# Rearranging keys and queries over the partitions: six and three copies, partly in place, instead of eight and four into new tiles

## The chip, the cores and the metric

The kernel runs on one core of a Trainium2 chip. The metric is the device time of one execution in microseconds (us). TensorE is called PE here, its weight loads PEld, VectorE DVE, ScalarE ACT, GpSimd POOL and SyncE SP. SP computes nothing: it issues DMA transfers from one queue, in order, and where one of them has to wait for a semaphore, SP waits with it.

## The reference

Two layers over 256 latent and 256 context tokens, width 1024. A layer is a half-step feed-forward block, a mix of three branches (neighbourhood attention, Fourier mixing, windowed grouped-query attention with sinks), and another half-step block. The part that the change touches is the two attentions:

```python
s_loc = jnp.einsum('brcqhd,brcwkhd->bhrcqwk', qg, kb).astype(jnp.float32) * scale + bias[None]
s_ctx = jnp.einsum('brcqhd,blhd->bhrcql', qg, kc).astype(jnp.float32) * scale
p = jax.nn.softmax(jnp.concatenate([s_loc, s_ctx], axis=-1), axis=-1)
...
w = window_gqa_attention(apply_rope(heads(wq, WA_HEADS), cos, sin), apply_rope(heads(wk, WA_KV_HEADS), cos, sin), ...)
```

There are eight heads of 64 channels in either attention, eight key heads in the first and two in the second. In the second layer only the latent tokens have queries.

## The kernel before

Everything is float32, but PE multiplies a rounded form of it. So each operand is split in two parts, `hi` (the rounded value) and `lo` (the rest), and a product is made of several matmuls: `mm3` (lines 293 to 295) does three for a projection, a score does two (lines 712 and 713).

Weights come as 424 blocks of 128x1024. For each, SP loads a `raw` tile (line 57, 512 KB), ACT makes `wh` (line 66), DVE or, inside attention, POOL makes `wl` (line 79). Five `raw` tiles are in rotation.

A projection of keys or queries gives a PSUM tile with two heads: the channels of one head in partitions 0 to 63 (called x in the code), those of the other in 64 to 127 (y). ACT writes its `hi` (line 876, or 896 behind the rotary embedding), DVE its `lo` (878 or 898). A score matmul contracts over 128 partitions, and the kernel fills them with both parts of one head: for queries a tile with `hi` above `lo`, for keys one tile with `hi` in both halves and one with `lo` in both halves. The first matmul of a score (712) multiplies the query tile by the `hi` keys, the second (713) by the `lo` keys. `stack` makes these tiles with DMA copies of 64 partitions from SBUF to SBUF (line 871): four for a pair of queries, eight for a pair of keys. Per layer there are five pairs of keys (four `nk`, one `wk`) and eight of queries (four `nq`, four `wq`).

Tiles of the tag `act` (activations, probabilities, `hi` and `lo` parts, stacked tiles, and temporaries named `tmp`) share 60 buffers. A new tile takes a buffer that an older one has left, and its first writer waits for the last reader of the old one.

The order of all instructions is written out by the program itself: `attention` walks through blocks of four scores, and between two steps `fill` puts in projection work according to a table of due times, and `pieces` runs the stages of the evacuations. The rotary embedding (`rope`) of `wk` and `wq` issues four small copies on SP (line 890), then three operations on POOL (893), then ACT (896), DVE (898) and `stack`. Loads of weights (57), of attention masks (697) and the copies all stand in SP's one queue in program order.

Of the kernel before, what the change touches and what calls it, by code (L numbers as in the profile page):

```python
# [7 lines left out]
F32 = mybir.dt.float32  # L8
# [255 lines left out]
class Emit:  # L264
# [568 lines left out]
    def mix(self, l, norm, nxt):  # L833
        nc, W = self.nc, self.W
        ctxq = l < DEPTH - 1
        n = NT if ctxq else NLAT
# [3 lines left out]
        u = norm.all()  # L840
# [4 lines left out]
        res, pending, later, items, spare, clock = {}, [], [], [], [], [0]  # L845
# [11 lines left out]
        def stack(name, hi, lo, n):  # L857


            a, b = self.act(), self.act()  # L860
            x, y = slice(0, 64), slice(64, 128)
            if "q" in name[0]:
                moves = (a, x, hi, x), (a, y, lo, x), (b, x, lo, y), (b, y, hi, y)
                res[name] = a, b
            else:
                c, d = self.act(), self.act()
                moves = ((a, x, hi, x), (a, y, hi, x), (b, x, hi, y), (b, y, hi, y),
                         (c, x, lo, x), (c, y, lo, x), (d, x, lo, y), (d, y, lo, y))
                res[name] = a, b, c, d
            for t, i, s, j in moves:  # L870
                nc.sync.dma_start(out=t[i, :n].bitcast(F32), in_=s[j, :n].bitcast(F32))

        def plain(scale):
            def evac(name, ps, n):
                hi, lo = self.act(), self.act()
                nc.scalar.activation(out=hi[:, :n], in_=ps[:, :n], func=AF.Copy, scale=scale)
                yield
                nc.vector.scalar_tensor_tensor(out=lo[:, :n], in0=ps[:, :n], scalar=scale,
                                               in1=hi[:, :n].bitcast(F32), op0=ALU.mult, op1=ALU.subtract)
                stack(name, hi, lo, n)  # L880
            return evac

        def rope(scale):
            def evac(name, ps, n):

                t, r = self.tmp()[:, :n], self.tmp()[:, :NLAT]
                nc.scalar.activation(out=t, in_=ps[:, :n], func=AF.Copy)
                for b in range(4):
                    o = 32 * (b ^ 1)
                    nc.sync.dma_start(out=r[32 * b:32 * b + 32], in_=t[o:o + 32, :NLAT])  # L890
                yield 2
                for x, y, z, op in ((t, t, self.cos, ALU.mult), (r, r, self.sin, ALU.mult), (t, t, r, ALU.add)):
                    nc.gpsimd.tensor_tensor(out=x[:, :NLAT], in0=y[:, :NLAT], in1=z, op=op)
                yield 1
                hi, lo = self.act(), self.act()
                nc.scalar.activation(out=hi[:, :n], in_=t, func=AF.Copy, scale=scale)
                yield 1
                nc.vector.scalar_tensor_tensor(out=lo[:, :n], in0=t, scalar=scale, in1=hi[:, :n].bitcast(F32),
                                               op0=ALU.mult, op1=ALU.subtract)
                stack(name, hi, lo, n)  # L900
            return evac
# [310 lines left out]
```

## Time and profile before

| | us |
|---|---|
| median of 3 runs | 2097.94 |
| lowest and highest | 2097.83, 2099.03 |
| the profiled execution | 2094.62 |
| its span | 2092.8 |
| PE busy in it | 2046.4 (98%) |
| DVE, ACT, POOL busy | 1269.2, 837.7, 370.0 |

The profiled execution is one execution of the program with the hardware profiler on; its span runs from its first to its last instruction, and all positions in this text are us from the start of that span. Layer 0 does its attention from about 485 to 650, layer 1 from about 1661 to 1775.

### The profile page before, as it was taken

To read this page: it belongs to the slowest core of one execution; us is meant where nothing else is said; L and a number is where in the kernel's file an instruction comes from. 1 tells how busy PE (TensorE), PEld (TensorE's weight loads), DVE (VectorE), ACT (ScalarE), POOL (GpSimd) and SP (SyncE) were. 2 spreads that over 40 slices of the span, in tenths; PEclk is the share of its full clock that TensorE was granted. 3 is DMA by queue.
4 is the path that set the end of the run, shared out by engine and by line. 5 is a ranking of instruction groups with operands and counts; after the bars stand their busy time and mean duration, and the time that the engine had idled before them with its cause. 6 is when DMAs were issued, how large, how long until landed. Compare 5 with 4: busy or idle time off the path is not lost.

```text
span 2092.8 us, 29113 instructions
## 1 busy us (share of the span) xinstructions
PE 2046.4 (98%) x11193; PEld 1764.3 (84%) x11193; DVE 1269.2 (61%) x2035; ACT 837.7 (40%) x1362; POOL 370.0 (18%) x373
## 2 busy tenths in 40 slices
PE   7999999999999999999999999999999999999998
PEld 3788888878887888988888898888888888999998
DVE  6777776565676335677777566533336558566554
ACT  4422222345787223442222243222224558645443
POOL 5200000402452111300000120000012157330002
PEclk8999999999999999999999999999999999999999
DMA  7456557445522333466666655633334474565553
GB/s 279 147 191 200 188 196 225 118 141 151 134 81 78 92 101 91 141 191 193 197 191 192 212 145 197 201 92 101 101 118 142 131 194 112 164 182 160 189 180 106
DMA packets 103011, 326.65 MB, mean 156 GB/s; under 512 B 13396, under 2 KB 18516, under 8 KB 102872
## 3 DMA queue, kind: packets, MB, share of 16 engines
q1 hardware_dynamic: 102872, 324.79, 50.0%
q8 instruction: 88, 1.44, 0.3%
q14 instruction: 51, 0.42, 0.1%
HBM read 305.60 MB, written 1.05 MB: 147 GB/s over the span
## 4 chain that ended last, share of the span: by engine, by line
PE 89%; DVE 5%; ACT 2%; DMA 1%; issue 1%; SPq 1%; POOL 1%; DVEq 0%; POOLq 0%; ACTq 0%
PE ps L294 27%; PE ps L295 27%; PE ps L293 27%; DVE dump L315 2%; PE ps L764 1%; PE ps L746 1%; PE ps L589 1%; PE ps L588 1%; PE ps L587 1%; DVE wl L79 1%; ACT wh L66 1%; PE ps L712 1%; PE ps L713 1%; ACT tmp L770 0%; DVE act L218 0%
## 5 line engine op out<-in xcount | busy, mean ns | idle before, releaser
L294 PE MATMUL ps<-act,wh 128*128 128x512 f32 (+1 forms) x3227 | 1121.6, 348 | 8.0 <-DVE act L233 7.3
L293 PE MATMUL ps<-act,wh 128*128 128x512 f32 (+1 forms) x3227 | 1122.6, 348 | 2.1 <-ACT act L212 1.1
L295 PE MATMUL ps<-act,wl 128*128 128x512 f32 (+1 forms) x3227 | 1120.5, 347 | 1.8 <-DVE wl L79 1.8
L294 PEld LDWEIGHTS ps<-act,wh 128*128 128x128 f32 x3227 | 613.7, 190 | 84.6 <-DVE act L233 8.8
L295 PEld LDWEIGHTS ps<-act,wl 128*128 128x128 f32 x3227 | 613.6, 190 | 77.5 <-DVE wl L79 2.6
L293 PEld LDWEIGHTS ps<-act,wh 128*128 128x128 f32 x3227 | 613.8, 190 | 77.0 <-ACT act L212 1.3
L66 ACT ACTIVATE wh<-raw 128x1024 fp32r<-128x1024 f32 x424 | 436.5, 1050 | 318.7 <-PE ps L294 283.3
L79 DVE TENSOR_TENSOR wl<-raw,wh 128x1024 fp32r<-128x1024 f32 x379 | 473.4, 1262 | 102.5 <-ACT wh L66 102.4
L315 DVE CUSTOM_DVE_ANT_0 dump<-ada,silu_row 128x1024 bf16<-128x1024 f32 x224 | 273.5, 1221 | 11.4 <-DMA ada<-in_w_ada 9.1
L302 ACT ACTIVATE act<-tmp 128x512 fp32r<-128x512 f32 (+1 forms) x122 | 66.8, 566 | 430.7 <-DVE tmp L517 412.5
L455 POOL TENSOR_TENSOR tmp<-h 128x512 f32<-128x512 f32 (+1 forms) x7 | 11.4, 1634 | 1121.3 <-DVE h L472 793.8
L472 DVE SCALAR_TENSOR_TENSOR h<-ps,mod,h 128x256 f32<-128x256 f32 x136 | 61.8, 481 | 200.0 <-PE ps L295 200.0
L517 DVE TENSOR_TENSOR tmp<-tmp,ps 128x512 f32<-128x512 f32 (+1 forms) x88 | 54.6, 620 | 206.3 <-PE ps L295 201.5
L79 POOL TENSOR_TENSOR wl<-raw,wh 128x256 fp32r<-128x256 f32 x180 | 142.5, 822 | 200.7 <-ACT wh L66 184.8
L303 DVE TENSOR_TENSOR act<-tmp,act 128x512 fp32r<-128x512 f32 (+1 forms) x122 | 74.3, 626 | 60.5 <-ACT act L302 60.5
L516 ACT ACTIVATE tmp<-ps 128x512 f32<-128x512 f32 (+1 forms) x88 | 47.8, 543 | 121.0 <-PE ps L295 120.3
L461 POOL TENSOR_TENSOR tmp<-h 128x256 f32<-128x256 f32 (+1 forms) x44 | 64.3, 1462 | 107.4 <-DVE h L472 103.0
L753 DVE TENSOR_TENSOR act<-ps,act 128x512 fp32r<-128x512 f32 x80 | 55.0, 687 | 33.8 <-ACT act L748 29.0
L724 ACT ACTIVATE tmp<-tmp,sm 128x512 f32<-128x512 f32 (+1 forms) x96 | 62.1, 647 | 31.5 <-DVE sm L722 30.0
L764 PE MATMUL ps<-act 128*128 128x256 f32 x320 | 61.6, 308 | 11.0 <-DVE act L753 9.4
L748 ACT ACTIVATE act<-ps 128x512 fp32r<-128x512 f32 x80 | 47.5, 594 | 45.9 <-PE ps L746 45.4
L1057 ACT ACTIVATE tmp<-ps 128x512 f32<-128x512 f32 (+1 forms) x30 | 15.4, 512 | 121.6 <-PE ps L295 121.6
(110 smaller groups left out, 1317.8 us busy)
## 6 DMA issues: line engine op xcount, KB each, us to landing
raw<-in_ws SPq DMA_DIRECT2D x424, 512.0 KB, 4.1
ada<-in_w_ada SPq DMA_DIRECT2D x128, 512.0 KB, 3.7
act<-act SPq DMA_DIRECT2D x112, 128.0 KB, 2.4
tmp<-in_w_ada_sc SPq DMA_DIRECT2D x16, 256.0 KB, 5.4
tmp<-in_w_ada SPq DMA_DIRECT2D x16, 256.0 KB, 6.0
masks<-in_na_bias SPq DMA_DIRECT2D x8, 512.0 KB, 5.0
h<-in_h SPq DMA_DIRECT2D x8, 256.0 KB, 5.3
act<-act SPq DMA_DIRECT2D x32, 64.0 KB, 4.2
```

The costliest lines, as they stand in the source:

```text
L66: self.nc.scalar.activation(out=wh, in_=self.raw[i], func=AF.Copy)
L79: self.lo_engine.tensor_tensor(out=wl[:, s], in0=raw[:, s], in1=self.hi[i][:, s].bitcast(F32), op=ALU.subtract)
L293: mm(ps, lhsT=w[0], rhs=x[0], start=start, stop=False)
L294: mm(ps, lhsT=w[0], rhs=x[1], start=False, stop=False)
L295: mm(ps, lhsT=w[1], rhs=x[0], start=False, stop=stop)
L302: nc.scalar.activation(out=hi, in_=src, func=AF.Copy)
L303: nc.vector.tensor_tensor(out=lo, in0=src, in1=hi.bitcast(F32), op=ALU.subtract)
L315: self.nc.vector.tensor_tensor_reduce(out=self.dump[:, ks], in0=w, in1=self.silu_row[:, v, ks], scale=1.0, scalar=m if half else 0.0, op0= ...
L461: nc.gpsimd.tensor_tensor(out=sq, in0=h, in1=h, op=ALU.mult)
L472: self.nc.vector.scalar_tensor_tensor(out=h, in0=ps, scalar=self.mod[l, g][:, v, j:j + 1], in1=h, op0=ALU.mult, op1=ALU.add)
L724: nc.scalar.activation(out=e[:, :nk], in_=e[:, :nk], func=AF.Exp, scale=-1.0, bias=nm, accum_out=b["sum"][:, i:i + 1])
L764: nc.tensor.matmul(b["ps"][hp][:, :256], lhsT=v, rhs=t[j][:, cs], start=c == 0 and j == 0, stop=c == n - 1 and j == 1)
```

## The change

`stack` keeps the two tiles that ACT and DVE wrote and uses them as half of its results. For a pair of queries it takes one new tile `b`, copies `hi`'s and `lo`'s lower half (y) into it, and then writes `lo`'s upper half over `hi`'s lower half; that third copy overwrites what the first one reads. For a pair of keys it takes two new tiles and does, once for `hi` and once for `lo`: lower half to the new tile's upper half, lower half to the new tile's lower half, then the old tile's upper half over its own lower half. Nothing else is changed.

```diff
-            a, b = self.act(), self.act()
             x, y = slice(0, 64), slice(64, 128)
+
+            def move(t, i, u, j):
+                nc.sync.dma_start(out=t[i, :n].bitcast(F32), in_=u[j, :n].bitcast(F32))
+
+            b = self.act()
             if "q" in name[0]:
-                moves = (a, x, hi, x), (a, y, lo, x), (b, x, lo, y), (b, y, hi, y)
-                res[name] = a, b
+                move(b, x, hi, y)
+                move(b, y, lo, y)
+                move(hi, y, lo, x)
+                res[name] = hi, b
             else:
-                c, d = self.act(), self.act()
-                moves = ((a, x, hi, x), (a, y, hi, x), (b, x, hi, y), (b, y, hi, y),
-                         (c, x, lo, x), (c, y, lo, x), (d, x, lo, y), (d, y, lo, y))
-                res[name] = a, b, c, d
-            for t, i, s, j in moves:
-                nc.sync.dma_start(out=t[i, :n].bitcast(F32), in_=s[j, :n].bitcast(F32))
+                d = self.act()
+                for t, u in ((hi, b), (lo, d)):
+                    move(u, x, t, y)
+                    move(u, y, t, y)
+                    move(t, y, t, x)
+                res[name] = hi, b, lo, d
```

In the kernel before, this stands in SP's queue at layer 0, from the `lo` copies of the second pair of keys (`act_3799` is their `lo` part, `act_3829` and `act_3830` the new tiles) over two weight loads to the copies of the second pair of queries. DMAHW0 to DMAHW7 are the semaphores that tell of landed transfers, given out in turn, so a wait for a single one is for the transfer eight earlier.

```order
L871 DMA act_3829<-act_3799 64x512 [waits DMAHW3_49,DVE_49,PE_49]
L871 DMA act_3829<-act_3799 64x512 [waits DMAHW4_49]
L871 DMA act_3830<-act_3799 64x512 [waits DMAHW5_49,PE_49]
L871 DMA act_3830<-act_3799 64x512 [waits DMAHW6_49]
L57 DMA raw_3844<-in_ws 128x1024 [waits DMAHW7_49,Pool_49]
L57 DMA raw_3900<-in_ws 128x1024 [waits DMAHW0_49,Activation_49,Pool_49]
L871 DMA act_3920<-act_3889 64x512 [waits DMAHW1_49,Activation_49]
L871 DMA act_3920<-act_3890 64x512 [waits DMAHW2_49,DVE_49]
L871 DMA act_3921<-act_3890 64x512 [waits DMAHW3_49,PE_49]
L871 DMA act_3921<-act_3889 64x512 [waits DMAHW4_49]
```

The same place of the changed kernel, on SP again, with all six copies of the keys (`act_3792` is their `hi`, `act_3793` their `lo`) and the three of the queries (`act_3879` is `hi`, `act_3880` `lo`):

```order
L863 DMA act_3821<-act_3792 64x512 [waits Activation_49]
L863 DMA act_3821<-act_3792 64x512
L863 DMA act_3792<-act_3792 64x512 [waits DMAHW5_49,DMAHW6_49,DMAHW4_49,DVE_49]
L863 DMA act_3822<-act_3793 64x512 [waits PE_49]
L863 DMA act_3822<-act_3793 64x512 [waits DMAHW0_49]
L863 DMA act_3793<-act_3793 64x512 [waits DMAHW7_49,DMAHW1_49,DMAHW0_49]
L57 DMA raw_3834<-in_ws 128x1024 [waits DMAHW2_49,Pool_49]
L57 DMA raw_3890<-in_ws 128x1024 [waits DMAHW3_49,Activation_49,Pool_49]
L863 DMA act_3910<-act_3879 64x512 [waits Activation_49]
L863 DMA act_3910<-act_3880 64x512 [waits DVE_49]
L863 DMA act_3879<-act_3880 64x512 [waits DMAHW6_49,DMAHW4_49]
```

Each copy in place (rows whose two tiles are `hi` or `lo` themselves) now waits for the landing of the copies just ahead of it, and what follows it in the queue, the weight loads among it, stands behind that wait; the order of the loads among the stacks is as it was.

The second place is DVE in layer 1, where the `lo` part of the first `wq` pair is made (line 898, 904 after the change), with the last mask step of a block (722) and the `lo` part of a transposed probability tile (753). Before:

```order
L722 ISA tmp_14134,sm_14118<-ps_14122,masks_282 128x512 [waits DMAHW3_49,DMAHW2_49,DMAHW4_49,DMAHW1_49,DMAHW5_49,DVE_49,PE_49]
L722 ISA sm_14118 128x1
L898 SCALAR_TENSOR_TENSOR act_14095<-tmp_13965,act_14094 128x256 [waits DMAHW5_49,DMAHW4_49,DMAHW6_49,DMAHW3_49,Activation_49]
L737 RECIPROCAL sm_13940<-sm_13938 128x2
L753 TENSOR_TENSOR act_14132<-ps_14126,act_14131 128x512 [waits DMAHW2_49,DMAHW1_49,DMAHW7_49,DMAHW0_49,Activation_49]
```

And the same place on DVE in the changed kernel:

```order
L722 ISA tmp_14070,sm_14054<-ps_14058,masks_282 128x512 [waits DMAHW3_49,PE_49]
L722 ISA sm_14054 128x1
L904 SCALAR_TENSOR_TENSOR act_14031<-tmp_13905,act_14030 128x256 [waits DVE_49,Activation_49]
L737 RECIPROCAL sm_13880<-sm_13878 128x2
L753 TENSOR_TENSOR act_14068<-ps_14062,act_14067 128x512 [waits DVE_49,PE_49,Activation_49]
```

Lines 898 and 753 wrote into buffers that stacking copies had still to read; in the changed kernel the tiles that they write wait for no copy.

## Rows read from the trace of the kernel before

**Rows 1.** The page: busy time of the engines.

```profile
PE 2046.4 (98%) x11193; PEld 1764.3 (84%) x11193; DVE 1269.2 (61%) x2035; ACT 837.7 (40%) x1362; POOL 370.0 (18%) x373
```

**Rows 2.** Busy time by stretch: us, then busy us (count) of PE, PEld, DVE, ACT and POOL, the granted clock of PE (1.00 is full speed), the DMA engines' busy share and GB/s.

```profile
1670.00:1760.00 90.00, 82.52 (x562) 74.98 (x560) 57.14 (x128) 60.54 (x139) 57.77 (x78) 0.98 0.63 171
1695.00:1700.00 5.00, 5.00 (x40) 4.57 (x39) 2.53 (x7) 4.10 (x8) 0.00 (x0) 1.00 0.99 384
1715.00:1720.00 5.00, 3.29 (x14) 3.19 (x15) 2.69 (x6) 1.08 (x3) 0.00 (x0) 0.66 0.72 190
```

**Rows 3.** The page's DMA issues: count, size of one, median us from issue to landing.

```profile
raw<-in_ws SPq DMA_DIRECT2D x424, 512.0 KB, 4.1
```

**Rows 4.** The stacking copies alone (tile `act`, engine SP): issue time on SP in ns, least, median and most; first and last issue in us.

```profile
L871 SPq DMA_DIRECT2D act<-act x144: 461/548/1682, 469.0 to 1755.3; - x144
```

**Rows 5.** The waits of PE from 510 to 1660 for parts of weights: total us, times, longest.

```profile
PE ps L588 <- DVE wl L79: 1.3, 1, 1.3
...
PE ps L295 <- DVE wl L79: 1.0, 2, 0.9
```

**Rows 6.** SP in order of time from 495 to 508, layer 0, the second pair: start, us, what, count.

```profile
495.46 0.33 SPq L697 DMA_DIRECT2D masks<-in_na_bias  x1
495.88 5.37 SPq L871 DMA_DIRECT2D act<-act  x8
501.35 1.03 SPq L57 DMA_DIRECT2D raw<-in_ws  x2
502.47 2.62 SPq L871 DMA_DIRECT2D act<-act  x4
```

**Rows 7.** Issue to landing (least, median, most) of stacking copies in four short stretches: 495.8 to 496.6 (the first two keys of rows 6, a mask load just ahead); 502.4 to 502.9 (the first queries of rows 6, two weight loads just ahead); 563.3 to 568 (the `wk` keys, nothing ahead); 1670.3 to 1670.7 (layer 1, one weight load just ahead).

```profile
DMA to landing us min/median/max: 5.1/5.1/5.2
DMA to landing us min/median/max: 5.6/5.6/5.6
DMA to landing us min/median/max: 2.3/2.3/2.3
DMA to landing us min/median/max: 4.6/4.6/4.6
```

**Rows 8.** PE in order of time: the first score of three blocks, the second `nq` pair of layer 0, the first `wq` pair of layer 0, the second `nq` pair of layer 1; in brackets idle us before it and what ended it.

```profile
508.85 0.47 PE L712 MATMUL ps<-act 128*128 128x512 f32 x1 [1.64 <-DMA act<-act]
575.05 0.47 PE L712 MATMUL ps<-act 128*128 128x512 f32 x1
1675.66 0.39 PE L712 MATMUL ps<-act 128*128 128x512 f32 x1
```

**Rows 9.** SP in order of time from 562.5 to 574, layer 0: the `wk` keys, a weight load, the first `wq` queries.

```profile
563.39 4.98 SPq L871 DMA_DIRECT2D act<-act  x8
568.48 0.52 SPq L57 DMA_DIRECT2D raw<-in_ws  x1
571.25 2.64 SPq L871 DMA_DIRECT2D act<-act  x4
```

**Rows 10.** SP in order of time from 1664 to 1710, layer 1: `nk` keys of the second pair, a load, its queries, a load, keys of the third pair, a load, a mask, queries, a load, the fourth pair's keys and queries in one row, three loads, a mask, the four rope copies of `wk`.

```profile
1664.65 4.95 SPq L871 DMA_DIRECT2D act<-act  x8
1669.65 0.59 SPq L57 DMA_DIRECT2D raw<-in_ws  x1
1670.35 2.61 SPq L871 DMA_DIRECT2D act<-act  x4
...
1673.69 5.27 SPq L871 DMA_DIRECT2D act<-act  x8
1679.05 0.54 SPq L57 DMA_DIRECT2D raw<-in_ws  x1
1679.68 0.39 SPq L697 DMA_DIRECT2D masks<-in_na_bias  x1
1680.16 2.41 SPq L871 DMA_DIRECT2D act<-act  x4
...
1683.29 9.58 SPq L871 DMA_DIRECT2D act<-act  x12
1692.96 1.51 SPq L57 DMA_DIRECT2D raw<-in_ws  x3
1696.14 0.33 SPq L697 DMA_DIRECT2D masks<-in_na_bias  x1
1698.19 2.45 SPq L890 DMA_DIRECT2D tmp<-tmp  x4
```

**Rows 11.** In order of time, engine by engine, what follows from the rope copies of rows 10, with the weight block that the load at 1679.05 feeds ahead of them on ACT: POOL's first rope operation, ACT's `hi` part of the first `wq` pair, ACT's next transposed tile, DVE's two operations of the second place shown above, the PE matmul that reads the last of them.

```profile
1687.27 1.06 ACT L66 ACTIVATE wh<-raw 128x1024 fp32r<-128x1024 f32 x1 [1.62 <-PE ps L294]
1702.05 0.74 POOL L893 TENSOR_TENSOR tmp<-tmp,cos 128x256 f32<-128x256 f32 x1 [8.51 <-DMA tmp<-tmp]
1710.00 0.42 ACT L896 ACTIVATE act<-tmp 128x256 fp32r<-128x256 f32 x1 [0.33 <-POOL tmp L893]
1711.27 0.58 ACT L748 ACTIVATE act<-ps 128x512 fp32r<-128x512 f32 x1
1713.30 0.55 DVE L898 SCALAR_TENSOR_TENSOR act<-tmp,act 128x256 fp32r<-128x256 f32 x1 [2.73 <-DMA act<-act]
1715.97 0.69 DVE L753 TENSOR_TENSOR act<-ps,act 128x512 fp32r<-128x512 f32 x1 [2.04 <-DMA act<-act]
1716.71 1.01 PE L764 MATMUL ps<-act 128*128 128x256 f32 x3 [3.19 <-DVE act L753]
```

## Prediction

> **What bounds the kernel now.** I read the page's engine totals first: PE is busy for 2046.4 us [rows 1] of a span of 2092.8, so only work that makes PE stand still, or that lowers its clock, can lengthen the kernel, and only PE's 46 idle us can be won. The change touches nothing but SP's queue, so the second view is the stacking copies alone: 144 of them, 548 ns of issue time each [rows 4]. The third is PE at the scores that read stacked tiles. One score waits for a copy today, 1.64 us at 508.85; the scores at 575.05 and 1675.66 show no wait [rows 8], but their query copies were issued only 2 to 4 us ahead (end of the last row of [rows 9], and 1670.35 + 2.61 = 1672.96 in [rows 10]). The last view is what follows the copies at the end of attention in layer 1: PE stands for 3.19 us at 1716.71 because DVE waited twice for copies, 2.73 and 2.04 us [rows 11], and in those 5 us PE's granted clock is 0.66, a mix of its two levels of 1.2 and 2.4 GHz, where it was 1.00 twenty us earlier [rows 2].
>
> **What is removed.** 36 of 144 issues, 36 x 0.55 = 20 us of SP's time over the kernel. SP is not PE: this counts only where a score or a load stands behind the copies. Also removed are the reuses of buffers that copies had still to read; at the second place shown of DVE the waits for DMA are gone from lines 898 and 753 (904 and 753 after).
>
> **What is added.** 36 waits of SP for a landing: two in each of 10 key pairs, one in each of 16 query pairs (the first and second layers alike). Let L be the time from the issue of the copy waited for to its landing. A copy is issued every 0.6 us [rows 4, 6]. For a pair of keys: first copy at 0, second at 0.6, landed at 0.6 + L, then third, fourth, fifth 0.6 apart, the fifth landed 2.3 after its issue at 4.1 + L, the sixth, and the next instruction 4.7 + L after the first. For queries the third copy waits for the landing of the first as far as its own issue goes: L, plus 0.6 for itself, and the pair is usable a further landing later. L is known from both sides: 2.3 with nothing ahead in the queue, 4.6 behind one weight load, 5.1 behind a mask load and 5.6 behind two weight loads [rows 7]. A weight load alone lands after 4.1 [rows 3], so a copy that is issued 0.6 us behind one should need at least about 3.6.
>
> So keys take SP 7.0 us when alone and 7.6 to 9.1 behind a load, instead of 4.95 [rows 10]; queries take 2.9 alone and 4.2 to 5.2 behind a load, instead of 2.6. Fewer issues, but more time in the queue, and for queries two landings in series before a score instead of one.
>
> **Place A, layer 0, second `nq` pair.** Before: keys from 495.88, two loads at 501.35, queries from 502.47 [rows 6], score at 508.85 [rows 8]. After: keys at 495.9 and 496.5, L = 5.1 (the same mask load is ahead), third at 501.6, fourth and fifth at 502.2 and 502.8, fifth landed at 505.1, sixth, loads at 505.7 and 506.3, queries at 506.9. Their first copy lands between 4.1 - 0.5 = 3.6 (no worse than the load just ahead of it) and 5.6 later, at 510.5 to 512.5; the third copy then takes 2.3: 512.8 to 514.8. The score is 4.0 to 6.0 us later. I take **+5.0**, the middle, since the first end lets the two loads go as fast as one.
>
> **Place B, layer 0, first `wq` pair.** Keys at 563.39, nothing ahead: 7.0, so the load stands at 570.4 instead of 568.48 and ends before the query's `hi` is ready; the first query copy stays at 571.25 [rows 9]. With L = 2.3 the third copy lands at 575.9; with the load now 0.85 us ahead, L is 4.1 - 0.85 = 3.3 to 4.6, and the third lands at 576.8 to 578.2. The score was at 575.05 [rows 8]: +0.9 to +3.1, taken **+2.0**, near the row of one load that has the queue to itself.
>
> **Place C, layer 1.** From 1664.65 SP issues three pairs of keys and three of queries almost without a pause, 4.95 + 2.61 + 5.27 + 2.41 + 9.58 = 24.8 us of copies. Then come three loads, a mask and the rope copies at 1698.19 [rows 10]. A load stands just ahead of four of the six groups. After: 7.0 + (4.2 to 5.2) + (7.6 to 9.1) + (4.2 to 5.2) + (7.6 to 9.1) + 2.9 = 33.5 to 38.5 us, 8.7 to 13.7 more. SP paused for 1.6 us ahead of the mask and 1.6 ahead of the rope copies, which take up to 3.2 of it: the rope copies come 5.5 to 10.5 us later, 13.7 if the pauses move along. I take 8. POOL waited for them until 1702.05, and ACT at 1710.00 for POOL [rows 11], so both move by 8. From there ACT's next transposed tile ended at 1711.85; with DVE's waits for copies gone, DVE and PE follow in 0.74 us (1715.97 to 1716.71 in [rows 11]), at 1712.6 + 8 = 1720.6 instead of 1716.71: **+3.9**, the slip less the 4.1 that the two waits cost today (+1.4 to +9.6 for slips of 5.5 to 13.7). The first score of this stretch also slips: keys 7.0, next issue 1671.65, query at 1672.25, first copy landed 3.6 to 4.6 later, third at 1678.2 to 1679.2 against 1675.66, 2.5 to 3.5 us. That is inside the +3.9, because the later wait is set by SP's chain and not by PE.
>
> **Clock.** The stretch at 1715 to 1720 lost 5 x (1 - 0.66) = 1.7 us [rows 2] behind a wait of 3.19. Place A becomes a wait of 1.64 + 5.0 = 6.6 us, so one such loss is added there; layer 1 had one and keeps one. **+1.7**, 0 if the clock stays, 3.4 if place C gets a second one.
>
> **What comes back.** Between A and C, PE waits 1.3 + 1.0 us for parts of weights [rows 5], which DVE could finish while PE stands. I take 0 and keep -2.3 as the end. The saved issues elsewhere are hidden behind PE.
>
> **Sum.** 5.0 + 2.0 + 3.9 + 1.7 = 12.6. The profiled execution took 2094.6 us, so its like would take 2107.2; the median of the runs shown is 3.3 higher, and on it 2097.9 + 12.6 = **2110.5**. Ends: 4.0 + 0.9 + 1.4 + 0 - 2.3 = 4.0, 2101.9; and 6.0 + 3.1 + 9.6 + 3.4 = 22.1, 2120.0.
>
> **Rivals.**
> (1) *No change: landings of 2.3 us whatever is ahead.* If the longer landings of [rows 7] are only the price of many copies queued together, and the third copies no longer have that, A costs nothing (queries at 504.0, third landed at 508.6, before 508.85), B 0.9, and C has 3 x 7.0 + 3 x 2.9 = 29.7 against 24.8, rope copies 4.9 later, 4.9 - 4.1 = +0.8. Sum 1.7: 2099.6. For it: the 2.3 with nothing ahead [rows 7]. Against it: 5.1 belongs to the first two copies of a group, with only a mask load ahead. The Trainium skill, "DMA: Bandwidth & Descriptors", section "Anatomy of one DMA — SWDGE (gpsimd) path", gives a fixed 2.0 us plus the bytes over 436 GB/s, for another issuing path than SP's; for 128 KB this would be 2.3 us, an estimate, and would make this rival come out. By that rule the trace agrees where nothing is ahead and disagrees behind loads, 4.6 to 5.6.
> (2) *Faster.* The removed waits are won and nothing takes their place: 1.64 at A, 3.19 in layer 1, 1.7 of clock: 6.5 us, 2091.4. It decides if the third copy at A lands before 507.2 (508.85 - 1.64), 5.6 us sooner than the early end worked out above, and the rope copies slip by less than 0.9. Against it: SP's order lists the landing waits for every third copy. For it: only that fewer copies queue.
> (3) *Much slower.* The late loads starve PE too. The load at 1679.05 stands behind 7.0 + 4.7 + 8.3 instead of 4.95 + 2.61 + 5.27, so about 7 us later, 1686.2, landed at 1690.3; ACT reads it at 1687.27 [rows 11]. The five `raw` tiles give slack for the next ones, but if ACT, whose order is fixed, holds its transposed tiles for 3 us at each of three such loads, that is 9 more, and one more stretch at half clock: 2121; with C at its upper end, 2127.
>
> **Chances.** Forecast (slower, +4 to +22) 0.65; rival 1 0.18; rival 2 0.07; rival 3 0.10. A difference of 0.2%, about 4.2 us, is what a measurement of this kernel can tell from none. Faster by more than that: rival 2 and a little of the mishaps of the sum, 0.08. Within it: rival 1 and the lowest end of the forecast, 0.19. Slower 0.73. The range 2099 to 2120 holds the forecast and rival 1, and leaves out rival 2, and rival 3.
>
> **What would show it.** In the changed kernel's profile: PE's first score at A at about 514 with 6.6 us of idle behind a copy; that at B at about 582 (577 and the 5 of A), idle 2; that of layer 1 3 us later than PE is by then, idle 3; SP waiting at line 863 for DMA, 36 times; POOL's first rope operation 8 us later than 1702.05, besides the 7 that A and B give; no wait of lines 904 and 753 for DMA; granted clock well under 1.00 just after A. It is wrong if L behind a load is 2.3 in the new order, if SP had pauses that I count as work, or if PE has other matmuls to do ahead of those scores.

## The result and the profile after

| | before | after |
|---|---|---|
| median, us | 2097.89 | 2122.39 |
| span of the profiled execution, us | 2092.8 | 2120.4 |
| PE busy in it, us | 2046.4 | 2058.9 |

The ratio is 1.0117 with a 95% interval of 1.0104 to 1.0130: the changed kernel is slower by 24.5 us. The sign was forecast, the size was not (12.6 us, range up to 2120). All ratios below are of executions at the usual clock; two of the twelve of one kernel (place B only, below) took 2529 and 2892 us at a granted clock of 0.75 and 0.65, and its numbers are without them.

The page of the changed kernel, engine totals, and its DMA issues, to be read against [rows 1, 3] (count, size, median us from issue to landing):

```profile
PE 2058.9 (97%) x11193; PEld 1771.8 (84%) x11193; DVE 1268.1 (60%) x2035; ACT 838.4 (40%) x1362; POOL 370.2 (17%) x373
raw<-in_ws SPq DMA_DIRECT2D x424, 512.0 KB, 4.2
act<-act SPq DMA_DIRECT2D x84, 128.0 KB, 2.3
```

The same 11193 matmuls keep PE busy 12.5 us longer. That part is clock, not waiting: the mean granted clock is 0.986 over the span, where it was 0.992. The rest of the 27.6 us between the spans, 15.1, is PE standing still. SP's waits for landings are new (total us, times, longest), one for each copy in place:

```profile
SPq L863 <- DMA act<-act: 77.6, 36, 4.6
```

PE at the first scores of the three places, to be read against [rows 8], with the idle time ahead of each in brackets:

```profile
514.81 0.80 PE L712 MATMUL ps<-act 128*128 128x512 f32 x1 [6.57 <-DMA act<-act]
586.79 0.47 PE L712 MATMUL ps<-act 128*128 128x512 f32 x1 [3.21 <-issue]
1690.50 0.47 PE L712 MATMUL ps<-act 128*128 128x512 f32 x1 [2.83 <-DMA act<-act]
```

All three waits that the forecast named are there. At the second the profile names no copy. The third query copy there was issued at about 584.5 (three copies in 5.24 us from 579.73, less one issue of 0.46), 2.3 us ahead of the score, and the third one of place A landed 2.2 us after its issue: the wait fits the copy, by this sum and not by a row. SP at place A, to be read against [rows 6] (start, us, what, count):

```profile
496.87 9.52 SPq L863 DMA_DIRECT2D act<-act  x6
506.49 1.03 SPq L57 DMA_DIRECT2D raw<-in_ws  x2
507.57 5.47 SPq L863 DMA_DIRECT2D act<-act  x3
```

Six copies hold the queue for 9.5 us where eight held it for 5.4. The load comes 9.62 us after the first key copy (forecast 9.8). Three query copies take 5.5 us instead of 2.6.

PE's granted clock after the waits, to be read against [rows 2] (stretch; us; busy and count of PE, PEld, DVE, ACT, POOL; clock; DMA share; GB/s):

```profile
515.00:520.00 5.00, 5.00 (x16) 4.22 (x17) 1.99 (x6) 2.73 (x5) 0.27 (x1) 0.50 0.22 85
585.00:590.00 5.00, 3.21 (x18) 2.81 (x19) 2.47 (x7) 1.48 (x4) 1.04 (x2) 1.00 0.45 101
1690.00:1695.00 5.00, 4.50 (x17) 3.80 (x18) 1.66 (x5) 1.76 (x3) 1.08 (x2) 0.66 0.59 157
1720.00:1725.00 5.00, 4.14 (x17) 3.35 (x17) 3.05 (x8) 3.57 (x10) 0.00 (x0) 0.67 0.97 365
1735.00:1740.00 5.00, 3.37 (x16) 3.37 (x16) 3.97 (x8) 3.88 (x7) 3.95 (x6) 0.53 0.63 136
1740.00:1745.00 5.00, 5.00 (x32) 4.56 (x32) 1.92 (x4) 1.66 (x5) 0.00 (x0) 0.79 0.32 104
1770.00:1775.00 5.00, 5.00 (x30) 4.56 (x30) 3.63 (x11) 3.17 (x10) 0.19 (x1) 0.71 0.25 56
```

With 5 x (1 - clock) for each: 2.5 + 0 + 1.7 + 1.65 + 2.35 + 1.05 + 1.45 = 10.7 us, against 1.7 in the one such stretch of the kernel before in its attention. As there, these values are means over stretches of a clock that is either 2.4 or 1.2 GHz; 0.50 is the lower level throughout.

SP in layer 1, place C, to be read against [rows 10]:

```profile
1676.51 7.09 SPq L863 DMA_DIRECT2D act<-act  x6
1683.64 0.58 SPq L57 DMA_DIRECT2D raw<-in_ws  x1
1684.33 4.53 SPq L863 DMA_DIRECT2D act<-act  x3
...
1689.53 9.10 SPq L863 DMA_DIRECT2D act<-act  x6
...
1699.80 5.36 SPq L863 DMA_DIRECT2D act<-act  x3
...
1705.84 12.36 SPq L863 DMA_DIRECT2D act<-act  x9
1718.24 1.55 SPq L57 DMA_DIRECT2D raw<-in_ws  x3
1719.85 0.42 SPq L697 DMA_DIRECT2D masks<-in_na_bias  x1
1720.37 2.45 SPq L896 DMA_DIRECT2D tmp<-tmp  x4
```

The copies take 7.09 + 4.53 + 9.10 + 5.36 + 12.36 = 38.4 us instead of 24.8. The two pauses ahead of the mask and of the rope copies are gone: SP goes from one of these rows to the next without a gap from 1676 to 1720, and 22.7 us in them are waits for landings. These stacks begin 11.9 us later than before (1676.51 against 1664.65), so layer 1 adds 27.6 - 11.9 = 15.7 us of the two spans' difference.

What follows, to be read against [rows 11], engine by engine: ACT, POOL's first rope operation and a later addition of its own (line 776), DVE, PE:

```profile
1719.71 0.60 ACT L748 ACTIVATE act<-ps 128x512 fp32r<-128x512 f32 x1 [4.09 <-DMA act<-act]
1727.44 0.74 POOL L899 TENSOR_TENSOR tmp<-tmp,cos 128x256 f32<-128x256 f32 x1 [17.46 <-PE ps L713]
1735.13 0.72 POOL L776 TENSOR_TENSOR tmp<-tmp 128x256 f32<-128x256 f32 x1
1735.89 0.69 DVE L753 TENSOR_TENSOR act<-ps,act 128x512 fp32r<-128x512 f32 x1 [4.26 <-POOL tmp L776]
1720.37 0.38 PE L764 MATMUL ps<-act 128*128 128x256 f32 x1 [2.94 <-ACT act L748]
1736.63 1.01 PE L764 MATMUL ps<-act 128*128 128x256 f32 x3 [5.21 <-DVE act L753]
1768.90 0.62 PE L764 MATMUL ps<-act 128*128 128x256 f32 x3 [3.34 <-DVE act L753]
```

The PE matmul that the profile names ahead of POOL's 1727.44 was long done. What came last were the rope copies, issued from 1720.37 on, with this time from issue to landing (least, median, most of four):

```profile
DMA to landing us min/median/max: 5.1/5.3/5.5
```

DVE's waits for copies (2.73 and 2.04 us in [rows 11]) are gone, as its order had shown. Two others stand in their place. ACT's transposed tile (748) takes a buffer that a stacking copy has still to release, 4.09 us, and PE stands for 2.94 of it. And DVE's `lo` part of a tile (753), one score ahead of the old wait, waits 4.26 us for POOL's addition at line 776, which stands behind the late rope operations and a weight part on POOL; PE stands for 5.21. The order shown ahead of the prediction covered two operations of DVE alone, and neither of these waits was looked for.

### The profile page after: what moved, and what is told of

Read it like the earlier page. It is cut to its first block, busy times and chain, and to the rows that moved or that the text cites. A ratio compares the mean times of both kernels' runs of the same rounds, so it can differ in the third digit from the quotient of the medians.

```text
span 2120.4 us, 29019 instructions
## 1 busy us (share of the span) xinstructions
PE 2058.9 (97%) x11193; PEld 1771.8 (84%) x11193; DVE 1268.1 (60%) x2035; ACT 838.4 (40%) x1362; POOL 370.2 (17%) x373
## 3 DMA queue, kind: packets, MB, share of 16 engines
HBM read 305.60 MB, written 1.05 MB: 145 GB/s over the span
## 4 chain that ended last, share of the span: by engine, by line
PE 87%; DVE 6%; ACT 3%; DMA 2%; issue 1%; POOL 1%; SPq 0%; DVEq 0%; ACTq 0%; POOLq 0%
PE ps L294 27%; PE ps L295 26%; PE ps L293 26%; DVE dump L315 2%; PE ps L764 1%; PE ps L746 1%; PE ps L589 1%; PE ps L588 1%; PE ps L587 1%; DVE wl L79 1%; DMA act<-act 1%; DMA ada<-in_w_ada 1%; PE ps L712 1%; PE ps L713 1%; ACT wh L66 1%
```

## Experiments

All are compared with the kernel before, measured on the same chip. The last column is the ratio's excess over 1, times 2098 us. "Split" kernels have no copy in place; they are explained at the end.

| kernel | ratio, 95% interval | us |
|---|---|---|
| queries in place only | 1.0052 (1.0040 to 1.0065) | +10.9 |
| keys in place only | 1.0074 (1.0060 to 1.0088) | +15.5 |
| one wait per key pair | 1.0060 (1.0047 to 1.0073) | +12.6 |
| own tile, no copy in place | 1.0007 (0.9998 to 1.0015) | +1.5 |
| place A only | 1.0029 (1.0018 to 1.0040) | +6.1 |
| place B only | 1.0019 (1.0010 to 1.0027) | +4.0 |
| layer 1 only | 1.0072 (1.0060 to 1.0084) | +15.1 |
| second pair of layer 1 only | 1.0020 (1.0011 to 1.0029) | +4.2 |
| layer 1 without that pair | 1.0054 (1.0042 to 1.0067) | +11.3 |
| third and fourth pairs of layer 1 | 1.0037 (1.0023 to 1.0051) | +7.8 |
| wk and wq of layer 1 | 1.0029 (1.0018 to 1.0041) | +6.1 |
| split evacuation everywhere | 1.0007 (0.9998 to 1.0016) | +1.5 |
| split at three stacks | 0.9975 (0.9963 to 0.9986) | -5.2 |
| split at two stacks | 0.9976 (0.9968 to 0.9985) | -5.0 |

### Is it the wait?

Theory 1 is that the loss is SP's wait for a landing ahead of each copy in place; the rival is anything else that the change moved (fewer buffers, other landings, the new order). The first kernel keeps the six and three copies in their places and takes away nearly all that makes them wait (SP's waits for such landings fall from 77.6 to 3.9 us). It pays for that with 26 more operations on ACT and 10 on DVE, and takes as many tiles as the kernel before:

```diff
-                move(hi, y, lo, x)
-                res[name] = hi, b
+                move(hi2, y, lo, x)       # x half of hi2 written by ACT beside hi
+                res[name] = hi2, b
...
-                    move(t, y, t, x)
+                    move(t2, y, t, x)     # x half of hi2, lo2 written by ACT, DVE
```

> The same six and three copies in the same places of SP's queue, but nothing is written in place: ACT (and DVE for the keys' small parts) writes the x half a second time into a tile of its own, and the third copy goes there. SP has no landing to wait for; ACT has one more operation per pair (0.4 to 0.6 us, 26 of them), DVE one more per key pair. Theory 1: the waits are all of the loss, so this is the kernel before with 36 issues fewer: 2091 to 2099. Rival (fewer tiles or other landings delay it even without the waits): above 2106.

Measured 2099.03, ratio 1.0007: 23 us of the 24.5 are gone, and what is left cannot be told from the kernel before. So the loss goes with the waits. As the number of tiles is back at the old one too, this kernel alone does not part the two; the next keeps the changed kernel's tiles. Nor does it give a price for 36 issues alone: 36 fewer of them, with the added operations, gain nothing. PE in this kernel, at place A and at the end of layer 1's chain:

```profile
509.64 0.50 PE L712 MATMUL ps<-act 128*128 128x512 f32 x1 [2.44 <-DMA act<-act]
1713.84 0.63 PE L764 MATMUL ps<-act 128*128 128x256 f32 x3 [0.34 <-DVE act L753]
```

The wait of 3.19 us of [rows 11] has shrunk to 0.34, as the buffers' part of rival 2 had it; the profile gives that back in smaller waits at the same line, 11.1 us in 18 over the whole kernel against 10.4 in 12, which I did not trace one by one.

The second kernel leaves the copies in place and shortens the waits:

```diff
-                for t, u in ((hi, b), (lo, d)):
-                    move(u, x, t, y)
-                    move(u, y, t, y)
-                    move(t, y, t, x)
+                move(b, x, hi, y)
+                move(b, y, hi, y)
+                move(d, x, lo, y)
+                move(d, y, lo, y)
+                move(hi, y, hi, x)
+                move(lo, y, lo, x)
```

> The whole change, but the six copies of a key pair in another order: the four that go into new tiles first, then the two in place. The landing of the first two then lies beside the issue of the next two. Theory 1: a key pair takes SP 4.7 us with nothing ahead and up to 6.9 behind a load, 2.3 less than with two waits; place A 2.3 earlier, place C 2.3 to 7 earlier: 2111 to 2118. Rival (what costs is the place of the waits ahead of the queries, or the buffers, not the time that SP stands): 2121 to 2124.

Measured 2110.18, just under theory 1's range: the loss halves, with the tiles as they were. So at least this half is the time that SP stands. Place A in it, SP and then PE's score, and SP's waits for landings:

```profile
497.16 7.27 SPq L863 DMA_DIRECT2D act<-act  x6
513.28 0.47 PE L712 MATMUL ps<-act 128*128 128x512 f32 x1 [4.75 <-DMA act<-act]
SPq L863 <- DMA act<-act: 51.2, 35, 4.2
```

The keys hold SP 2.25 us less (7.27 against 9.52), PE's wait is 1.8 shorter, and 26 us less are waited for on SP in all.

### Keys or queries?

The stacks of one kind are done as in the kernel before (`a`, `c` new tiles, four or eight copies), the others in place.

```diff
-                for t, u in ((hi, b), (lo, d)):
-                    move(u, x, t, y)
...
+                a, c = self.act(), self.act()
+                for t, u, v in ((hi, a, b), (lo, c, d)):
+                    move(u, x, t, x)
+                    move(u, y, t, x)
+                    move(v, x, t, y)
+                    move(v, y, t, y)
```

> Queries in place (three copies), keys copied into four new tiles as in the kernel before (eight copies). Theory 1 (what costs is SP's wait for a landing, and each late score adds to the ones before it): a query pair becomes usable one landing later, and its SP time grows from 2.6 to 4.2-5.2 us behind a load. Place A: 502.5 + 5.6 + 2.3 = 510.4 against 508.85, +1.6; place B +0.9 to +3.1; place C +1.6 for the first score and some 3 us for the rope copies. Sum about +9, 5 to 14 with clock: 2103 to 2112. Rival (the keys' waits make nearly all of it, by delaying loads): within 3 us of the kernel before, under 2101.

> Keys in place (six copies, two waits), queries copied into new tiles as in the kernel before. Theory 1: keys hold SP 7.1 to 9.1 us instead of 4.95, so queries behind them start later: place A +4.4 and clock 2.5; place B 0; place C 2 for the first score, then 2 to 4 us for each of two further pairs. Sum about +13, 8 to 18: 2106 to 2116. If the two halves add up, the excess of this kernel and that of the one with queries alone make the 24.5 us of the whole change; if one score waits for the later of two delays, they make more.

Measured 2108.04 and 2113.01. Both fall in theory 1's ranges; the rival for the queries (under 2101) is out. Together they make 26.4 us against 24.5 of the whole change: nearly additive.

### Which places?

In place only where a condition on layer and name holds, for example place A:

```diff
-            if "q" in name[0]:
+            if "q" in name[0] and not (l == 0 and name[0] in ("nk", "nq") and name[1] == 1):
+                a = self.act()
+                move(a, x, hi, x)
...
```

> In place only for the second nk pair and the second nq pair of layer 0 (place A); all other stacks as in the kernel before. In the profile after, the score there came 4.9 us later and the 5 us behind it ran at half clock (2.5 us more). Theory 1 (the delays are local and add up): +7.4, 2104 to 2107, and PE's wait ahead of that score 6.6 us with a clock of about 0.5 behind it. Rival (part of it comes back later in gaps of PE, or part of it came from the buffers of the other stacks): +3 or less, 2099 to 2101.

> In place only for the wk pair and the first wq pair of layer 0 (place B). Theory 1: a wait of 3.2 us ahead of the first score of the wq pair, as after the whole change, and no drop of the clock behind it: +3.3, 2100 to 2102. Rival (the wait of 3.2 is owed to other late stacks and not to this place): below 1 us, 2097 to 2099.

> In place in layer 1 only; layer 0 as in the kernel before. Theory 1: the share of layer 1 in the profiles, 27.6 - 11.9 = 15 to 16 us: 2111 to 2115, with the same chain of delays (first score of the second nq pair 4.7 with clock, rope copies and reused buffers 7.5, a last 3.0). Rival (layer 1 runs late partly because layer 0 did): 8 or less, below 2106.

Measured 2104.19, 2101.54 and 2113.78. Place A is a little under 7.4, which its interval (3.8 to 8.4 us) holds; layer 1 as expected; together 6.1 + 4.0 + 15.1 = 25.2 against 24.5. Place B misses in one point. Its score and the clock, first place A's stretch for comparison, then B's score and stretch:

```profile
515.00:520.00 5.00, 5.00 (x18) 4.22 (x17) 1.99 (x6) 2.73 (x5) 0.71 (x2) 0.55 0.24 79
579.36 0.76 PE L712 MATMUL ps<-act 128*128 128x512 f32 x1 [3.46 <-issue]
580.00:585.00 5.00, 5.00 (x17) 4.16 (x16) 3.50 (x7) 1.48 (x4) 2.33 (x3) 0.50 0.38 118
```

The wait is 3.46 us and the clock falls to 0.50 behind it, where after the whole change a wait of 3.21 at the same place left the clock at 1.00. Wait and clock would make 6.0 us, more than the 4.0 of the ratio. The executions of this kernel lie between 2100.0 and 2105.9, so the clock may fall behind this wait in some and not in others; one profile cannot show that.

### Does the first delay of layer 1 vanish in the later one?

The prediction let the later wait of place C swallow that of its first score. Two kernels divide layer 1 along this line:

```diff
-            if "q" in name[0]:
+            if "q" in name[0] and not (l == 1 and name[0] in ("nk", "nq") and name[1] == 1):
...
```

and the same with `l == 1 and (name[0][0] == "w" or name[1] != 1)`.

> In place only for the second nk pair and the second nq pair of layer 1, where the changed kernel's profile has a wait of 2.8 us ahead of the first score and 1.7 us of clock behind it. The prediction held that this delay is swallowed by the later one of the rope copies. Theory 1 (it is not: the copies that follow in SP's queue wait for ACT, ACT for PE, so they slip with PE and the delay stays to the end): +4 to +5, 2101.5 to 2103.5. The prediction's reading (the wait of 3.19 us later in layer 1 shrinks by as much): 0 to +1.5, 2097 to 2100.

> In place in layer 1, but not for the second nk pair and the second nq pair. With layer 1 alone the excess was 15.3 us. Theory 1 (the delays of this layer add up): 15.3 - 4.5 = 10.8, 2107 to 2111. The prediction's reading (the rope copies' lateness counts from the start of the copies, not from PE): 14 or more, 2112 and up, if the third and fourth pairs alone make them late; if all three pairs are needed for it, 6 or less.

Measured 2101.97 and 2109.04: 4.2 + 11.3 = 15.5 against 15.1 for layer 1. The delay of the second pair stays to the end, alone and beside the others. The score, the stretch behind it, and SP ahead of the rope copies in the first of the two kernels:

```profile
1680.93 0.62 PE L712 MATMUL ps<-act 128*128 128x512 f32 x1 [2.28 <-DMA act<-act]
1680.00:1685.00 5.00, 4.07 (x13) 3.35 (x14) 1.66 (x5) 1.76 (x3) 0.41 (x1) 0.66 0.93 222
1699.27 1.51 SPq L57 DMA_DIRECT2D raw<-in_ws  x3
1703.08 0.33 SPq L697 DMA_DIRECT2D masks<-in_na_bias  x1
1705.13 2.45 SPq L912 DMA_DIRECT2D tmp<-tmp  x4
```

2.28 of wait and 1.7 of clock make 4.0. SP's pauses ahead of the mask (1699.27 + 1.51 to 1703.08, 2.3 us) and ahead of the rope copies (1.7) are as long as before, 1.7 and 1.7 in [rows 10], or longer. They don't take up any of it: the mask waits for DVE and the rope copies for ACT, and both follow PE, as theory 1 had it. In the whole of layer 1 SP has no pause left, and there the second pair's 4.1 us of queue (7.09 + 4.53 against 4.95 + 2.61) would count by way of SP as well; that the two kernels add up does not say which way it went.

### The rest of layer 1

The third and fourth `nk` and `nq` pairs alone (`name[0][0] == "n" and name[1] >= 2`), and `wk` and `wq` alone (`name[0][0] == "w"`), both with `l == 1`:

> In place only for the third and fourth nk and nq pairs of layer 1. Theory 1 (these hold SP, so that the rope copies behind them in the queue come late, and ACT waits for a buffer that a copy of the fourth pair has still to read): most of the 11.6 us that layer 1 cost without its second pair, +8 to +11: 2105.5 to 2108.5, with waits of PE at lines 764 of 2.9 and some 5 us. Rival (the wk and wq stacks themselves make the most of it): +5 or less.

> In place only for the wk and wq stacks of layer 1. Theory 1: the stacks behind the rope copies add only the last wait of about 3 us with what of it is new (1.5 to 3): 2099 to 2100.5; and DVE's waits for copies of the kernel before may be gone (-3). Rival: +6 or more.

Measured 2106.80 and 2104.49. The first falls where theory 1 had it (7.8 by the ratio, at the lower end). The second meets its rival, +6: I had given the `wk` and `wq` stacks too little. The wait of the first on ACT, with what it made PE wait; then two waits of the second on PE, with the stretch behind the later one:

```profile
1708.05 0.60 ACT L748 ACTIVATE act<-ps 128x512 fp32r<-128x512 f32 x1 [5.42 <-DMA act<-act]
1708.69 0.39 PE L764 MATMUL ps<-act 128*128 128x256 f32 x1 [4.27 <-ACT act L748]
```

```profile
1726.51 0.47 PE L712 MATMUL ps<-act 128*128 128x512 f32 x1 [1.47 <-DMA act<-act]
1750.92 1.00 PE L764 MATMUL ps<-act 128*128 128x256 f32 x3 [3.34 <-DVE act L753]
1750.00:1755.00 5.00, 4.08 (x17) 3.78 (x18) 3.79 (x9) 1.27 (x4) 1.61 (x3) 0.50 0.36 120
```

ACT's wait for a buffer belongs to the third and fourth pairs: it is there with these alone in place. The `wk` and `wq` stacks of layer 1 have late scores of their own, and a wait of 3.34 us with half clock behind it that the changed kernel has too (at 1768.90). 7.8 + 6.1 = 13.9 against 11.3 for both: these two overlap by 2.6 us, near their joint uncertainty, and what of that is real stays open.

### A version without the waits

A half that stays in its partitions needs no copy at all if ACT and DVE write it where it is used:

```diff
+            a, b = self.act(), self.act()
+            for t, i in (a, x), (b, y):
+                nc.scalar.activation(out=t[i, :n], in_=src[i, :n], func=AF.Copy, scale=scale)
...
+            for t, h, i in (c, a, x), (d, b, y):      # d is c for queries
+                nc.vector.scalar_tensor_tensor(out=t[i, :n], in0=src[i, :n], scalar=scale, in1=h[i, :n].bitcast(F32),
+                                               op0=ALU.mult, op1=ALU.subtract)
+            if "q" in name[0]:
+                move(a, y, c, x)
+                move(b, x, c, y)
+                res[name] = a, b
+            else:
+                for t, i, j in (a, y, x), (b, x, y), (c, y, x), (d, x, y):
+                    move(t, i, t, j)
+                res[name] = a, b, c, d
```

> ACT and DVE write the x half and the y half of a part into the two tiles where each is used (two operations of 64 partitions in the place of one of 128), so that only halves that have to change their partitions are copied: four copies for a pair of keys, two for queries, none in place, no landing to wait for. SP issues 72 copies in the place of 144; ACT and DVE have one operation more per part (0.4 to 1.2 us, 26 each). Theory 1: place A's wait of 1.64 us, layer 1's waits of DVE for copies (3.19 on PE) and the 1.7 us of clock behind them go: 2089 to 2096, faster than both. Rival (the doubled operations of ACT and DVE delay the evacuations by more than the copies save): 2098 to 2106.

> Kernel before, with the split evacuation (halves written where they are used, four and two copies) at three stacks only: second nk and nq pair of layer 0, and wk of layer 1, whose copies PE waits for in the kernel before (1.64 us; and 3.19 us through DVE's reused buffers, with 1.7 of clock). With the split at all stacks these waits were gone, but PE was late by some 1 us at each of six other places. Theory 1 (those are the added operations of ACT and DVE at the other stacks): 1.4 + 4.7 less about 1: 2092 to 2094.5. Rival (they come with the changed places of buffers, whatever the added operations): 2096 to 2099.

> As the kernel with three split stacks, but with the second nq pair of layer 0 left as before: two split stacks. Theory 1: the key pair of four copies ends 2.4 us of SP time sooner, enough for the score at 508.85 (wait of 1.64): the same 2092 to 2094.5. Rival: that wait is of the query copies' own landing behind the two loads, and stays: 1.6 more than with three split stacks.

Everywhere, it measured 2099.34, a miss: not faster. At three stacks 2092.51 and at two 2092.37, both clearly faster than the kernel before. Halving the copies everywhere did not pay; halving those that PE waited for did. What takes the gain back at the other stacks was not tested by itself: the split adds 26 operations on ACT and 26 on DVE, and it also moves the buffers. The added operations are not cheap. One of ACT's on 64 partitions is no shorter than one on 128 (median 590 ns against 578; count, least, median, most; the kernel before, then the split everywhere):

```profile
L876 ACT ACTIVATE act<-ps x16: 362/578/600, 468.3 to 1683.4; 128x512 fp32r<-128x512 f32 x12, 128x256 fp32r<-128x256 f32 x4
L861 ACT ACTIVATE act<-ps x32: 363/590/595, 468.9 to 1691.6; 64x512 fp32r<-64x512 f32 x24, 64x256 fp32r<-64x256 f32 x8
```

Place A and the end of layer 1's chain in the kernel with two split stacks (its lines 713 and 765 are 712 and 764), and the stretch that had clock 0.66:

```profile
508.13 0.39 PE L713 MATMUL ps<-act 128*128 128x512 f32 x1
1710.26 0.62 PE L765 MATMUL ps<-act 128*128 128x256 f32 x3 [0.85 <-DVE act L754]
1715.00:1720.00 5.00, 5.00 (x42) 4.74 (x41) 3.90 (x10) 4.33 (x13) 3.06 (x4) 1.00 0.38 120
```

The 1.64 us ahead of the score, 2.3 of the 3.19 and the 1.7 of clock are gone: 5.7 us, against 5.0 measured. The rival to the second kernel (the wait at 508.85 is of the query copies' own landing) is out: it vanished with the keys alone split. I would put the split only into these two stacks.

## Why the prediction was wrong, step by step

**The mechanism was right, and the sign with it; what failed is the step on place C in layer 1, and with it the size of the clock's term.** SP waits 36 times for a landing, the loads and queries behind it come late, PE waits at the three scores named, and the clock falls. Rival 1 (landings of 2.3 us whatever is ahead) is refuted at place A, where two loads stand ahead and SP could issue the third query copy only 5.0 us after the first (the 5.47 us of the three, less one issue of 0.46 as in [rows 4]), and in layer 1, where the first two query copies behind one load landed after this long (least, median, most):

```profile
DMA to landing us min/median/max: 4.0/4.1/4.2
```

Here the row decides against the 2.3 us that the prediction had estimated for 128 KB from the Trainium skill, "DMA: Bandwidth & Descriptors", section "Anatomy of one DMA — SWDGE (gpsimd) path". Rival 2 (faster) fell with it. Rival 3 named the right region (2121 to 2127), but for a reason that the profile does not show: PE has no new wait for a part of weights, and ACT waits for no weight load in layer 1; PE's new waits behind ACT and DVE come by way of stacking and rope copies.

**Place A**: forecast +5.0 and 1.7 of clock. The wait rose from 1.64 to 6.57, +4.9, but all of the 5 us behind it ran at half clock: 2.5. Right in the wait, 0.8 short in the clock.

**Place B**: forecast +2.0, bounds 0.9 to 3.1. Measured 3.2 after the whole change and 4.0 alone, just above the upper bound. The value taken was too low: the first query copy stood 0.75 us behind a load and took 4.7 us to land, where 2.3 to 4.6 was allowed.

**Place C** is where the step failed: forecast 3.9, measured 15.7 in the profile and 15.1 alone. Its first score was 2.8 us late, as forecast (2.5 to 3.5). The other terms of that step were wrong, all in one direction. How the 15.7 divide can be read from PE's busy time over the same work of layer 1, after and then before:

```profile
1676.00:1800.00 124.00, 107.82 (x692) 96.73 (x691) 70.08 (x156) 75.92 (x174) 69.92 (x93) 0.93 0.45 127
1664.10:1772.50 108.40, 100.55 (x688) 91.69 (x688) 70.14 (x155) 75.20 (x174) 69.78 (x92) 0.98 0.59 160
```

PE stands for 124.0 - 107.8 = 16.2 us instead of 7.9, 8.3 more, where 3.9 were forecast. It is busy for about 7 us more with the same matmuls (to within four), all of it clock, where the forecast kept the one loss of before and added none.

First, the slip of the rope copies. I let SP's pauses take up to 3.2 us and settled on 8. The copies came out at the upper end (38.4 of 33.5 to 38.5), and the rope copies 1720.37 - 1676.51 = 43.9 us after the first key copy, where 33.5 before: 10.3. POOL then started 7.1 us after their first issue instead of 3.9, because three loads, a mask and the rope copies now stand back to back (365 GB/s in the stretch from 1720). That is a slip of 13.5 us where 8 was taken and 13.7 was the far end.

Second, the credit of 4.1 us for DVE's vanished waits. By the forecast's own rule the slip of 13.5 makes 13.5 - 4.1 = 9.4. The waits did vanish, but the buffers that were reused in the new order brought the two others, 4.09 on ACT and 4.26 on DVE, and PE had little of the credit left. That a wait for a buffer is gone at one instruction says nothing on which instruction gets the next late buffer; for that the order of ACT and the waits for POOL had to be read too.

Third, the delay of the first score was let vanish in the later one. Alone it cost 4.2 us and stayed to the end, since SP's pauses follow PE and took up none of it; in the whole change it may be a part of the slip above.

Fourth, the stacks of `wk` and `wq` in layer 1 were taken as hidden. Alone they cost 6.1 us. In the profile after, PE waits 3.34 us at 1768.90 and loses 1.45 of clock behind it.

**Clock**: one more stretch of 1.7 us was forecast. By the table of stretches it is 10.7 against 1.7, 9.0 more; the page's busy time of PE says 12.5, of which 2.0 lie ahead of place A, nearly all in the first 70 us, which the change does not touch. Of the rest, the 2.5 at place A stand on the path by themselves. In layer 1, where SP's queue and POOL set the pace, some of it would have been waiting otherwise, so it is a part of the 15.7 and not a further term beside it.

So place A with its clock (7.4), B (3.2) and C (15.7) make 26.3 of the 27.6 us between the two profiled spans, about 1 more lies ahead of the first score, and the medians differ by 24.5. The lack of the forecast, 11.9, is C's almost alone. Open is how the 11.3 us of layer 1 without its second pair divide: the two halves cost 7.8 and 6.1 by themselves.

## What to carry to other kernels

On an in-order DMA queue a copy in place saved an issue of 0.55 us here and bought a wait of 2.2 us on average (77.6 us in 36) and 4.6 at most for the queue, and a second landing in series for its reader. Price the landing by what stands ahead of it in the queue and not by the copy's size alone: the same 128 KB landed in 2.2 to 2.3 us with nothing ahead and in 4.0 to 5.6 behind loads. Let a queue's pauses, or a later wait, swallow a delay only if what sets them does not itself follow the delayed engine; and count a buffer wait as gained only after looking which instruction on any engine gets the next late buffer. And price a wait of PE together with the clock behind it: from place A on, about 10 of the 27.6 us were clock (12.5 less the 2.0 ahead of it). Before cutting transfers everywhere, find the two or three that something waits for: two split stacks gave 5 us, all 26 gave none.

## What the runs showed of the hardware

A wait of PE is not paid for when it ends: behind waits of 2.3 to 6.6 us the mean of PE's granted clock was 0.50 to 0.71 over the 5-us stretch at the wait's end, in most places (1.45 to 2.5 us lost in each). It is not a matter of the wait's length alone: 3.21 us at place B left it at 1.00, 3.46 at the same score in another kernel brought it to 0.50, and 2.28 in layer 1 brought it to 0.66.
